# Storing the activation sums of a Strassen MLP in its up phase, loading operands in place, and moving the embedding projection between plain chunks

## The chip, the cores and the metric

One core of one Trainium2 chip. The metric is the device time of one execution of the program in microseconds (us). Three executions of the kernel before were timed.

## What is computed

One layer of a decoder trunk, for 512 tokens of width 2048, all in f32:

```
u  = rmsnorm(x);  x = x + gla(u)             # gated linear attention, 4 heads, output projection w_out
u  = rmsnorm(x);  z = relu(u @ w_up) ** 2    # 2048 -> 8192
x  = x + z @ w_down                          # 8192 -> 2048
u  = rmsnorm(x);  x = x + sigmoid(u @ w_ple_gate) * (p @ w_ple_proj)
out = rmsnorm(x)
```

`p` is an embedding of width 256 for each token. The GLA stage has its own input projections (q, k, v, output gate and a low-rank decay gate).

## The kernel before

**Arithmetic.** Every f32 operand is split into a high part in a reduced format (fp32r, a cast on ACT) and the remainder (a subtraction on DVE). A product is then three matmuls: high by high, high by remainder, remainder by high (mm3, L148 to L151). Weights are loaded by SP into a tile raw, cast on ACT to whi (L139) and subtracted on DVE to wlo (L141). The pools for these tiles have 3 raw, 4 whi, 4 wlo and 2 ld buffers; activations live in a pool of 34 slots of 4 KB per partition. The engines take their instructions in order, each from a queue of its own; a scheduler sets the order of the rows from the program's order.

**Stages**, by the trace: q, k and the low-rank gate of head 0 with the transposes of x (0 to 77 us); v, output gate, attention (to 652); the output projection wo, 8 groups of 4 weight chunks, whose results go through evac_out (L731 to L752; to 840); up (848 to 1503); the embedding projection and the first down groups (1503 to 1570); down (to 2230); the gate with the final norm (to the end).

**Start.** x_load (L242) loads 256 columns of x by SP; x_tile (L246) transposes 128 of them on PE. x_load(c+1) is issued when the tiles of x_load(c) are begun (L340).

**Output projection.** For each of 16 row tiles i, evac_out adds the residual xres (loaded by POOL from xT_d), writes the scaled u, adds the square to acc, stores h to DRAM (h_d), and builds the operands of the up phase for each pair kp of tiles: XS (sums) and XA (L709 to L725). The pairs 5 and 6 keep their u in a tile u_late, which is taken from the raw pool (L737) and held until after the projection.

**Up and down by a 2x2 Strassen scheme** with 7 products instead of 8. A weight chunk of 4 x 256 (chunk_sums, L796) gets its sums on DVE (L801, L804, L805); a chunk is 2 x 7 x 3 = 42 matmuls of 256 columns. In up there are 32 groups of 4 chunks; the 7 products of a group go to 4 banks and are added in combine (L825 to L836) into a tile e of 8 parts, of which 4 are the result. hidden (L838) applies Relu and Square and stores the four parts to DRAM (z_d, two stores by POOL).

Down works on slices of 4, 3, 3, 3, 3 chunks of the 16 that z has, as the slots hold no more; each slice has 8 groups g. Groups 0, 3 and 7 are PLAIN: ordinary products, 24 matmuls of 512 columns for each chunk (plain_chunk, L882); the others are Strassen groups. build (L896) makes the operands of one chunk: for two tiles kp it loads z into an ld buffer (POOL, L900), then hidden_operands (L867) casts z to Zh and subtracts to Zl, forms the four differences zd in the one tile d (L872 to L874), and splits these to Zdh and Zdl. After each group the partial h is loaded from h_d, added to and stored again (residual_in, L845, and residual_out, L852).

**The order around the change.** The main loop (L966 on) walks over the list work. At the first down chunk it builds the chunks 0 and 1 and runs the four parts of the embedding projection (project_embedding, L932; 4 x 24 matmuls; results leave through raw buffers named pp, copied by ACT at L941 and stored by ACT at L942). After group 2 of a slice one chunk of the next slice is built, where the slots allow; the rest is built chunk by chunk in group 0 of that slice. The steps that follow a group (combine, stores) are put into the list todo and flushed after the second chunk of the next one. rest_of_scale (L763) forms the token sums of acc (ps_ts_mlp) after the third up chunk.

Of the kernel before, what the change touches and what calls it, by code (L numbers as in the profile page):

```python
# [9 lines left out]
F32 = mybir.dt.float32  # L10
# [50 lines left out]
def trunk_kernel(ctx, tc, a, out):  # L61
# [63 lines left out]
    z_d = dram.tile([NG, P, 2, T], F32, name="z_d")  # L125
    pp_d = dram.tile([NTT, P, D], F32, name="pp_d")
# [184 lines left out]
    x_load(1)  # L311
    x_squares(0)
    ready = 2
    for k in range(NK):
# [351 lines left out]
    def spare_tile(shape, name):  # L666
        return mpool.tile(shape, F32, tag="d", name=name)

    def temp(name):
        return spare_tile([P, T], name)  # L670
# [4 lines left out]
    acc2 = mpool.tile([P, T], F32, tag="acc2", name="acc2")  # L675

# [51 lines left out]
    late = {}  # L728
    XOPS = [None] * NKP

    def evac_out(i, ps):  # L731
# [12 lines left out]
        h = late["x"][:, i % 2, :]  # L744
        nc.vector.tensor_tensor(out=h, in0=ps, in1=h, op=ALU.add)
        nc.vector.scalar_tensor_tensor(
            out=late["u"][:, i % 2, :], in0=h, scalar=vec("norm_mlp", i), in1=rb, op0=ALU.mult, op1=ALU.mult)
        add_squares(h, f"mlp_{i}", i == 0)
        if i % 2:
# [10 lines left out]
    f2 = mpool.tile([P, T], F32, tag="f2", name="f2")  # L760
    g2 = mpool.tile([P, T], F32, tag="g2", name="g2")

    def rest_of_scale():  # L763
        ssum = token_sums(acc2, "mlp")
        ms = tiny([P, NTT], "ms2")
        nc.vector.tensor_scalar(out=ms, in0=ssum, scalar1=1.0 / D, scalar2=EPS, op0=ALU.mult, op1=ALU.add)
        r = rstd_of(ssum, D, NTT, "mlp")
        f = tiny([P, NTT], "f")
        nc.vector.tensor_tensor(out=f, in0=r, in1=rinv, op=ALU.mult)
        ft = tiny([P, NTT], "ft")  # L770
        nc.vector.tensor_tensor(out=ft, in0=f, in1=f, op=ALU.mult)
        bcast(ft, f2, "f2")
# [23 lines left out]
    def chunk_sums(w, k4, g, name):  # L796
# [9 lines left out]
        return raw  # L806

# [17 lines left out]
    def combine(ps, name):  # L825
# [10 lines left out]
        return e[:, 0:4, :].rearrange("p (f h) t -> p f (h t)", f=2)  # L836

    def hidden(g, ps):  # L838
        z = combine(ps, f"up{g}")
        nc.scalar.activation(out=z, in_=z, func=AF.Relu)  # L840
        nc.scalar.activation(out=z, in_=z, func=AF.Square)
        for f in range(2):
            nc.gpsimd.dma_start(z_d[g, :, f, :], z[:, 1 - f, :])

    def residual_in(s_, g):  # L845
        hs = load([P, 2, T], f"h_{s_}_{g}")
# [5 lines left out]
    def residual_out(s_, g, hs):  # L852
        if s_ == len(SLICES) - 1:
            nc.vector.tensor_tensor(out=hs, in0=hs, in1=f2.unsqueeze(1).broadcast_to([P, 2, T]), op=ALU.mult)
        nc.gpsimd.dma_start(h_d[g], hs)

    def add_slice(s_, g, ps):
        z = combine(ps, f"dn{s_}_{g}")
# [275 lines left out]
```

## Time and profile before

| | |
|---|---|
| median of 3 executions | 2419.46 us (2417.47 to 2421.09) |
| the profiled execution | 2423.99 us, its span 2422.2 us |
| mean granted clock of TensorE | 0.984 of full speed |
| PE | busy 2361.6 us, 97% |
| DVE | busy 1690.2 us, 70% |
| ACT | busy 977.5 us, 40% |
| POOL | busy 152.5 us, 6% |
| DMA | 341.09 MB, 141 GB/s on the mean |

PE is TensorE, DVE is VectorE, ACT is ScalarE, POOL is GpSimd, SP is SyncE. PE's busy time holds matmuls of 256 and 512 columns; two may overlap in the records, so that the pace of a stretch is read from its length and its number of matmuls. An idle engine is of interest where PE waits for it.

### The profile page before, as it was taken

The numbers are of one execution on the slowest core, as the hardware profiler recorded it, in microseconds if no ns is written. First come the engines' busy times: TensorE is split into PE (matmuls) and PEld (weight loads), VectorE is DVE, ScalarE is ACT, GpSimd is POOL, SyncE is SP. The second block draws the span as 40 slices with busy tenths as digits, with TensorE's granted clock in tenths as the row PEclk, the third lists the DMA queues.
The fourth block names the chain that finished last, engine by engine and source line by source line (L and its number), as shares of the span: only waits on it lengthen the run. The fifth ranks groups of instructions, "written<-read, shape, count | busy, mean of one in ns | idle before, by whom it ended". The sixth has DMA issues, their size and how long they took to land.

```text
span 2422.2 us, 36477 instructions
## 1 busy us (share of the span) xinstructions
PE 2361.6 (97%) x14778; PEld 2136.3 (88%) x14778; DVE 1690.2 (70%) x2579; ACT 977.5 (40%) x1216; POOL 152.5 (6%) x282
## 2 busy tenths in 40 slices
PE   7999999999999899999999999899999999999998
PEld 6888888888878699999999998699898989899887
DVE  5654736547464588888888888578887888878435
ACT  4433424324332344444444446334433334434333
POOL 2000000000000000000000000000101010100000
PEclk8999999999999899999999999899999999999999
DMA  8333323332433344444444444545555565655433
GB/s 252 97 88 94 87 79 96 95 94 85 127 130 113 122 124 146 132 131 131 132 131 131 131 131 142 184 149 170 191 179 195 187 203 178 215 191 190 149 114 113
DMA packets 247753, 341.09 MB, mean 141 GB/s; under 512 B 13732, under 2 KB 202336, under 8 KB 247584
## 3 DMA queue, kind: packets, MB, share of 16 engines
q1 hardware_dynamic: 213072, 228.68, 31.0%
q0 software_dynamic: 30240, 105.75, 12.6%
q10 hardware_dynamic: 4272, 4.33, 0.6%
q8 instruction: 115, 1.88, 0.3%
q14 instruction: 54, 0.44, 0.1%
HBM read 281.05 MB, written 57.67 MB: 140 GB/s over the span
## 4 chain that ended last, share of the span: by engine, by line
PE 78%; issue 8%; DVE 5%; DMA 4%; ACT 1%; POOL 0%; ACTq 0%; DVEq 0%; POOLq 0%
PE ps_up L822 9%; PE ps_up L819 9%; PE ps_up L821 9%; PE ps_d L821 5%; PE ps_d L819 5%; PE ps_d L822 4%; DMA z<-z_d 3%; PE ps_wo L151 2%; PE ps_v L149 2%; PE ps_wo L149 2%; PE ps_v L150 2%; PE ps_og L150 2%; PE ps_v L151 2%; PE ps_og L149 2%; PE ps_og L151 2%
## 5 line engine op out<-in xcount | busy, mean ns | idle before, releaser
L811 ACT CAST whi_up<-raw_up 128x896 fp32r<-128x896 f32 x256 | 239.8, 940 | 317.5 <-PE ps_up L821 309.5
L813 DVE TENSOR_TENSOR wlo_up<-raw_up,whi_up 128x896 fp32r<-128x896 f32 x256 | 277.7, 1087 | 92.9 <-ACT whi_up L811 92.9
L819 PE MATMUL ps_up<-XS,whi_up 128*128 128x256 f32 x1024 | 290.4, 284 | 0.0
L821 PE MATMUL ps_up<-XS,whi_up 128*128 128x256 f32 x1024 | 290.4, 284 | 0.0
L822 PE MATMUL ps_up<-XS,wlo_up 128*128 128x256 f32 x1024 | 290.0, 284 | 0.0
L811 ACT CAST whi_d<-raw_dn 128x896 fp32r<-128x896 f32 x160 | 149.0, 942 | 241.1 <-PE ps_d L821 141.8
L819 PE MATMUL ps_up<-XA,whi_up 128*128 128x256 f32 x768 | 218.6, 285 | 3.7 <-ACT whi_up L811 3.7
L822 PE MATMUL ps_up<-XA,wlo_up 128*128 128x256 f32 x768 | 218.1, 284 | 0.5 <-DVE wlo_up L813 0.5
L821 PE MATMUL ps_up<-XA,whi_up 128*128 128x256 f32 x768 | 217.8, 284 | 0.0
L813 DVE TENSOR_TENSOR wlo_d<-raw_dn,whi_d 128x896 fp32r<-128x896 f32 x160 | 172.9, 1087 | 35.6 <-ACT whi_d L811 34.8
L819 PEld LDWEIGHTS ps_up<-XS,whi_up 128*128 128x128 f32 x1024 | 197.4, 193 | 0.0
L821 PEld LDWEIGHTS ps_up<-XS,whi_up 128*128 128x128 f32 x1024 | 197.3, 193 | 0.0
L822 PEld LDWEIGHTS ps_up<-XS,wlo_up 128*128 128x128 f32 x1024 | 197.1, 193 | 0.0
L821 PE MATMUL ps_d<-Zdl,whi_d 128*128 128x256 f32 x640 | 181.1, 283 | 0.0
L819 PE MATMUL ps_d<-Zdh,whi_d 128*128 128x256 f32 x640 | 181.1, 283 | 0.0
L822 PE MATMUL ps_d<-Zdh,wlo_d 128*128 128x256 f32 x640 | 181.1, 283 | 0.0
L150 PE MATMUL ps_d<-Zl,whi_d 128*128 128x512 f32 x384 | 151.9, 396 | 5.0 <-DVE Zl L876 5.0
L149 PE MATMUL ps_d<-Zh,whi_d 128*128 128x512 f32 x384 | 151.7, 395 | 3.9 <-ACT whi_d L139 2.2
L151 PE MATMUL ps_d<-Zh,wlo_d 128*128 128x512 f32 x384 | 151.5, 394 | 0.5 <-DVE wlo_d L141 0.5
L819 PEld LDWEIGHTS ps_up<-XA,whi_up 128*128 128x128 f32 x768 | 147.9, 193 | 4.2 <-ACT whi_up L811 3.9
L822 PEld LDWEIGHTS ps_up<-XA,wlo_up 128*128 128x128 f32 x768 | 148.0, 193 | 0.9 <-DVE wlo_up L813 0.8
L821 PEld LDWEIGHTS ps_up<-XA,whi_up 128*128 128x128 f32 x768 | 148.0, 193 | 0.2 <-issue 0.2
(345 smaller groups left out, 6057.9 us busy)
## 6 DMA issues: line engine op xcount, KB each, us to landing
raw_up<-in_w_up SPq DMA_DIRECT2D x128, 512.0 KB, 3.8
raw_dn<-in_w_down SPq DMA_DIRECT2D x80, 512.0 KB, 3.7
raw_d<-in_w_down SPq DMA_DIRECT2D x48, 512.0 KB, 3.8
h<-h_d POOLq DMA_DIRECT2D x40, 512.0 KB, 4.6
h_d<-h POOLq DMA_DIRECT2D x40, 512.0 KB, 3.0
raw_v<-in_gla_w_in SPq DMA_DIRECT2D x32, 512.0 KB, 3.8
raw_og<-in_gla_w_in SPq DMA_DIRECT2D x32, 512.0 KB, 3.7
raw_wo<-in_gla_w_out SPq DMA_DIRECT2D x32, 512.0 KB, 3.4
```

The source lines that it names most:

```text
L149: nc.tensor.matmul(ps, lhsT=wa[0], rhs=wb[0], start=first, stop=False)
L150: nc.tensor.matmul(ps, lhsT=wa[0], rhs=wb[1], start=False, stop=False)
L151: nc.tensor.matmul(ps, lhsT=wa[1], rhs=wb[0], start=False, stop=last)
L811: nc.scalar.copy(hi[:, 1:8, :], raw[:, q_, 1:8, :])
L813: nc.vector.tensor_tensor(out=lo[:, 1:8, :], in0=raw[:, q_, 1:8, :], in1=hi[:, 1:8, :].bitcast(F32), op=ALU.subtract)
L819: nc.tensor.matmul(dst, lhsT=hi[:, wb, :], rhs=xh, start=first and q_ == 0 and half == 0, stop=False)
L821: nc.tensor.matmul(dst, lhsT=hi[:, wb, :], rhs=xl, start=False, stop=False)
L822: nc.tensor.matmul(dst, lhsT=lo[:, wb, :], rhs=xh, start=False, stop=last and q_ == 1 and (b == 3 or half == 1))
```

## The change

- **Start.** x_load is one tile of x further ahead.
- **Output projection.** The tile u_late is gone: the pairs 5 and 6 are scaled in place in xres (pair 5 in a new buffer ld2), after h is stored. The square is taken before the scaling. The first raw tile of the up phase is loaded and summed at i = 13, ahead of the last groups' end. The tile f2 shares the buffer of acc.
- **Up.** After Relu and Square, hidden_sums forms the four differences on DVE in the free parts of e, and a third store per group puts them to a new DRAM tile zd_d (512 KB). todo gives out one step per chunk.
- **Operands.** hidden_operands is replaced by split: the load goes into the slot of the remainder, ACT casts it into the high part's slot, and DVE subtracts in place. The parts Zu (from z_d) and Zd (from zd_d) are built separately; the plain groups need Zu only. Builds for the next slice come after groups 2, 6 and 7; 32 more loads of 512 KB go by POOL.
- **Embedding projection.** Its part i comes after plain chunk i of the first down group, and its results leave through the ld and ld2 buffers.

The diff's core:

```diff
@@ start
-                if ready % 2 == 0 and ready // 2 + 1 < NK // 2:
-                    x_load(ready // 2 + 1)
+                if ready % 2 == 0 and ready // 2 + 2 < NK // 2:
+                    x_load(ready // 2 + 2)
@@ evac_out
-            late["x"] = load([P, 2, T], f"xres_{kp}")
+            late["x"] = (load2 if kp == 5 else load)([P, 2, T], f"xres_{kp}")
...
-            if kp == 5:
-                late["s"] = wtile([P, 2, 2, T], "raw", "u_late")
             if kp in (5, 6):
-                late["u"] = late["s"][:, kp - 5, :, :]
+                late["u"] = late["x"]
...
         if i % 2:
             nc.gpsimd.dma_start(h_d[kp], late["x"])
+            if kp in (5, 6):
+                for j in range(2):
+                    scale_out(i - 1 + j, late["x"][:, j, :])
+            if i == 13:
+                first_raw.append(raw_of(0))
@@ up
+    def hidden_sums(g, e):
+
+        for o, x, y in ((4, 2, 3), (5, 3, 1), (6, 2, 5), (7, 0, 6)):
+            nc.vector.tensor_tensor(out=e[:, o, :], in0=e[:, x, :], in1=e[:, y, :], op=ALU.subtract)
+        nc.gpsimd.dma_start(zd_d[g], e[:, 4:8, :])
@@ operands
+    def split(src, kp, name):
+
+        h, l = (slot([P, 4, HT], f"Z{name}{n}_{kp}", F32R) for n in ("h", "l"))
+        nc.gpsimd.dma_start(l.bitcast(F32), src)
+        nc.scalar.copy(h, l.bitcast(F32))
+        nc.vector.tensor_tensor(out=l, in0=l.bitcast(F32), in1=h.bitcast(F32), op=ALU.subtract)
+        return h, l
@@ main loop
-            if s_ == 0 and g == 0 and first:
-                for i in range(4):
-                    build_to(i // 2 + 1)
-                    project_embedding(i)
             if g == 0:
                 build_to(k4 + 1)
+            if g == 1:
+                build_sums_to(k4 + 1)
...
                 plain_chunk(ps, k4, g, first, last, f"{name}_{k4}")
+                if s_ == 0 and g == 0:
+                    flush()
+                    build_to(min(k4 + 2, end))
+                    project_embedding(k4)
+                    build_sums_to(k4 + 1)
...
-            if g == 2 and last and 8 * (SLICES[s_] + 1) <= 34:
-                build_to(end + 1)
+            if last and end < NG // 2:
+                if g == 2 and SLICES[s_] == 3:
+                    build_to(end + 2)
+                if g == 6:
+                    build_to(end + 3)
+                if g == 7:
+                    build_sums_to(end + 1)
         if todo and not first:
-            flush()
+            todo.pop(0)()
```

**ACT at the end of group 5 of the output projection** (sq_mlp are the squares that wait for the group's results, whi_wo6 the weight casts of the group that follows). Before:

```order
L682 ACTIVATE sq_mlp_8_5333<-xres_4_5328 128x512
L682 ACTIVATE sq_mlp_9_5338<-xres_4_5328 128x512
L714 CAST XS0_4_5342<-u_4_5330 128x1024
L722 CAST XA0_4_5344<-u_4_5330 128x256
L722 CAST XA0_4_5344<-u_4_5330 128x512
L682 ACTIVATE sq_mlp_10_5482<-xres_5_5477 128x512
L682 ACTIVATE sq_mlp_11_5487<-xres_5_5477 128x512
L722 CAST XA0_4_5344<-u_late_5479 128x256
L139 CAST whi_wo6_0_5495<-raw_wo6_0_5493 128x1024
L139 CAST whi_wo6_1_5525<-raw_wo6_1_5523 128x1024
```

With the change:

```order
L684 ACTIVATE sq_mlp_8_5333<-xres_4_5329 128x512
L684 ACTIVATE sq_mlp_9_5338<-xres_4_5329 128x512
L140 CAST whi_wo6_0_5495<-raw_wo6_0_5493 128x1024
L716 CAST XS0_4_5343<-u_4_5331 128x1024
L724 CAST XA0_4_5345<-u_4_5331 128x256
L724 CAST XA0_4_5345<-u_4_5331 128x512
L140 CAST whi_wo6_1_5525<-raw_wo6_1_5523 128x1024
L140 CAST whi_wo6_2_5555<-raw_wo6_2_5553 128x1024
L140 CAST whi_wo6_3_5585<-raw_wo6_3_5583 128x1024
L684 ACTIVATE sq_mlp_10_5481<-xres_5_5478 128x512
L684 ACTIVATE sq_mlp_11_5485<-xres_5_5478 128x512
```

The four casts of group 6 have moved ahead of the squares of pair 5.

**ACT in the embedding projection** (whi_wp are its weight casts, pp its results, Zh and Zdh the casts of operands; whi_d0_1_0_0 belongs to the first chunk of down group 1). Before:

```order
L942 DMA pp_d_110<-pp_0_1_13431 128x2x512
L139 CAST whi_wp1_13451<-raw_wp1_13449 128x1024
L841 ACTIVATE e_up31_13665<-e_up31_13665 128x1024
L871 CAST Zh_4_13679<-z_4_13676 128x1024
L875 CAST Zdh_4_13681<-zd_4_13678 128x1024
L871 CAST Zh_5_13693<-z_5_13690 128x1024
L941 COPY pp_1_0_13455<-ps_ple1_0_0_13456 128x512
```

With the change, at the projection's end:

```order
L978 COPY pp_3_1_13897<-ps_ple3_1_0_13898 128x512
L978 COPY pp_3_1_13897<-ps_ple3_1_1_13906 128x512
L911 CAST Zdh_6_13915<-Zdl_6_13916 128x1024
L979 DMA pp_d_111<-pp_3_1_13897 128x2x512
L844 CAST whi_d0_1_0_0_13934<-raw_dn1_0_13838 128x896
L844 CAST whi_d0_1_0_1_13959<-raw_dn1_0_13838 128x896
L911 CAST Zdh_7_13920<-Zdl_7_13921 128x1024
L911 CAST Zuh_8_15226<-Zul_8_15227 128x1024
L844 CAST whi_d0_1_1_0_13989<-raw_dn1_1_13925 128x896
```

Before, Zh and Zdh stand between the weight casts and the copies from the first part on; with the change the operands that the next chunk does not need stand at the end, around the casts of group 1.

**POOL from up to down** (z_d and zd_d are the stores of the last up groups, Zul and Zdl the loads into the slots). Before:

```order
L843 DMA z_d_109<-e_up30_13263 128x512 x2
L900 DMA z_2_13491<-z_d_109 128x1024
L900 DMA z_3_13505<-z_d_109 128x1024
L900 DMA z_4_13676<-z_d_109 128x1024
L900 DMA z_5_13690<-z_d_109 128x1024
L843 DMA z_d_109<-e_up31_13665 128x512 x2
L900 DMA z_6_13739<-z_d_109 128x1024
```

With the change:

```order
L910 DMA Zul_3_13598<-z_d_109 128x1024
L910 DMA Zdl_0_13645<-zd_d_110 128x1024
L876 DMA z_d_109<-e_up31_13576 128x512 x2
L910 DMA Zdl_1_13650<-zd_d_110 128x1024
L883 DMA zd_d_110<-e_up31_13576 128x1024
L910 DMA Zul_4_13685<-z_d_109 128x1024
L910 DMA Zul_5_13690<-z_d_109 128x1024
L910 DMA Zdl_2_13737<-zd_d_110 128x1024
L910 DMA Zdl_3_13742<-zd_d_110 128x1024
L910 DMA Zul_6_13777<-z_d_109 128x1024
L910 DMA Zul_7_13782<-z_d_109 128x1024
```

The loads of z go out as before around the last stores, and those of zd stand between them.

## Rows read from the trace of the kernel before

**Rows 1.** The page: the span, and PE's line of busy time, share and instructions.

```profile
span 2422.2 us, 36477 instructions
PE 2361.6 (97%) x14778; PEld 2136.3 (88%) x14778; DVE 1690.2 (70%) x2579; ACT 977.5 (40%) x1216; POOL 152.5 (6%) x282
```

**Rows 2.** Waits of PE: line, releaser: us in total, times, longest us.

```profile
PE ps_xT L249 <- DMA x<-in_x: 8.0, 3, 4.1
PE ps_ple L149 <- ACT whi_wp L139: 7.6, 3, 2.8
PE ps_wo L149 <- ACT whi_wo L139: 5.0, 2, 4.1
PE ps_d L150 <- DVE Zl L876: 5.0, 4, 2.2
PE ps_up L819 <- ACT whi_up L811: 3.7, 2, 2.6
PE ps_ts_mlp L215 <- DVE acc L683: 3.6, 1, 3.6
```

**Rows 3.** Stretches: us, busy (count) of PE, PEld, DVE, ACT, POOL, clock, DMA, GB/s.

```profile
51.20:59.40 8.20, 4.12 (x15) 3.12 (x14) 2.00 (x4) 2.12 (x7) 1.24 (x2) 0.50 0.81 265
145.30:193.80 48.50, 48.50 (x230) 40.87 (x229) 26.91 (x47) 17.64 (x21) 0.00 (x0) 1.00 0.27 76
787.50:800.50 13.00, 7.92 (x20) 5.61 (x19) 7.64 (x13) 4.60 (x6) 1.28 (x2) 0.61 0.48 161
840.20:855.20 15.00, 8.27 (x41) 7.87 (x41) 14.83 (x28) 6.82 (x11) 1.33 (x2) 0.66 0.33 105
858.00:1480.00 622.00, 622.00 (x5176) 621.02 (x5175) 508.60 (x788) 298.21 (x339) 33.57 (x62) 1.00 0.43 132
968.90:1017.30 48.40, 48.40 (x406) 48.40 (x405) 39.89 (x62) 22.80 (x27) 2.17 (x4) 1.00 0.40 123
1505.50:1551.00 45.50, 31.17 (x90) 22.24 (x89) 25.82 (x30) 23.05 (x29) 3.77 (x7) 0.77 0.67 221
1727.50:1735.50 8.00, 5.20 (x15) 3.62 (x14) 6.46 (x10) 2.94 (x4) 0.53 (x1) 0.79 0.42 142
1857.00:1865.00 8.00, 5.11 (x14) 3.50 (x14) 6.06 (x9) 3.04 (x4) 0.53 (x1) 0.79 0.50 171
```

**Rows 4.** SP's timeline, 33-51 us: start, us, operation, [idle before <- releaser].

```profile
33.22 14.87 SPq L137 DMA_DIRECT2D raw_v<-in_gla_w_in  x3
48.14 2.01 SPq L244 DMA_DIRECT2D x<-in_x  x3
```

**Rows 5.** DMAs: tile, engine, count, KB each, median us to landing.

```profile
x<-in_x SPq DMA_DIRECT2D x8, 512.0 KB, 7.5
z<-z_d POOLq DMA_DIRECT2D x32, 512.0 KB, 4.4
```

**Rows 6.** ACT's timeline at 790 us and at 847 us.

```profile
790.81 1.99 ACT L139 CAST whi_wo<-raw_wo 128x1024 fp32r<-128x1024 f32 x2
846.88 0.93 ACT L811 CAST whi_up<-raw_up 128x896 fp32r<-128x896 f32 x1
```

**Rows 7.** DVE's and ACT's timelines in the up phase, 1121 to 1124 us.

```profile
1121.68 1.09 DVE L813 TENSOR_TENSOR wlo_up<-raw_up,whi_up 128x896 fp32r<-128x896 f32 x1 [0.90 <-ACT whi_up L811]
1122.82 0.94 ACT L811 CAST whi_up<-raw_up 128x896 fp32r<-128x896 f32 x1 [1.18 <-PE ps_up L821]
```

**Rows 8.** By tile (zd, z, e_up): count: duration ns min/median/max, first and last start.

```profile
L873 DVE TENSOR_TENSOR zd<-z,zd x32: 415/419/427, 892.4 to 2111.0; 128x256 f32<-128x256 f32 x32
L900 POOL DMA_DIRECT2D z<-z_d x32: 528/528/548, 886.8 to 2106.0; - x32
L843 POOL DMA_DIRECT2D z_d<-e_up x64: 540/540/557, 880.7 to 1510.9; - x64
```

**Rows 9.** POOL's timeline at 1507 us.

```profile
1507.06 0.53 POOL L900 DMA_DIRECT2D z<-z_d  x1 [4.31 <-DVE Zl L876]
```

**Rows 10.** ACT's timeline at 1727 us.

```profile
1727.37 1.05 ACT L871 CAST Zh<-z 128x1024 fp32r<-128x1024 f32 x1 [3.95 <-DMA z<-z_d]
```

More of the change, by code (lines that the diff above doesn't have):

```diff
@@ L125, in trunk_kernel @@
     z_d = dram.tile([NG, P, 2, T], F32, name="z_d")
+    zd_d = dram.tile([NG, P, 4, HT], F32, name="zd_d")
     pp_d = dram.tile([NTT, P, D], F32, name="pp_d")
@@ L675, in trunk_kernel, with load2 @@
     acc2 = mpool.tile([P, T], F32, tag="acc2", name="acc2")
+    def load2(shape, name):
+        return mpool.tile(shape, F32, tag="ld2", name=name)
     def add_squares(src, name, first):
@@ L725, in operands, with chunk_sums, raw_of, scale_out @@
         return ops
+    w_up = a["w_up"].rearrange("o k c -> (o k) c")
+    w_dn = a["w_down"].rearrange("o k c -> (o k) c")
+    B11, T1, T3, B22, B21, T2, T4 = range(1, 8)
+    PRODUCTS = ((A11, B11), (R2, T2), (S3, T3), (S1, T1), (A12, B21), (R4, B22), (A22, T4))
+    BANK = ((0, 0), (0, 1), (1, 0), (1, 1), (2, 0), (2, 1), (3, 0))
+    def chunk_sums(w, k4, g, name):
+        raw = wtile([P, 2, 8, P], "raw", f"raw_{name}")
+        rows = raw.rearrange("p q (k b n) c -> p (q k) b (n c)", k=2, b=2)
+        nc.sync.dma_start(rows[:, :, 0, :], w_rows(w, 4 * k4, 4, 256 * g, 256))
+        tc.keep_in_program_order(nc.vector.tensor_tensor(
+            out=raw[:, :, 2:4, :], in0=raw[:, :, 1:5:3, :], in1=raw[:, :, 0:1, :].broadcast_to([P, 2, 2, P]),
+            op=ALU.add))
+        nc.vector.tensor_tensor(out=raw[:, :, 6, :], in0=raw[:, :, 2, :], in1=raw[:, :, 4, :], op=ALU.add)
+        nc.vector.tensor_tensor(out=raw[:, :, 7, :], in0=raw[:, :, 6, :], in1=raw[:, :, 5, :], op=ALU.add)
+        return raw
+    work = []
+    for g in range(NG):
+        for k4 in range(NK // 4):
+            work.append((0, g, k4, k4 == 0, k4 == NK // 4 - 1))
+    c0 = 0
+    for s_, nc_ in enumerate(SLICES):
+        for g in range(NKP):
+            for j in range(nc_):
+                work.append((1 + s_, g, c0 + j, j == 0, j == nc_ - 1))
+        c0 += nc_
+    def raw_of(n):
+        if n >= len(work):
+            return None
+        stage, g, k4, _, _ = work[n]
+        if stage == 0:
+            return chunk_sums(w_up, k4, g, f"up{g}_{k4}")
+        if g not in PLAIN:
+            return chunk_sums(w_dn, k4, g, f"dn{g}_{k4}")
     late = {}
     XOPS = [None] * NKP
+    first_raw = []
+    def scale_out(i, h):
+        nc.vector.scalar_tensor_tensor(
+            out=late["u"][:, i % 2, :], in0=h, scalar=vec("norm_mlp", i), in1=rb, op0=ALU.mult, op1=ALU.mult)
     def evac_out(i, ps):
@@ L745, in evac_out @@
         nc.vector.tensor_tensor(out=h, in0=ps, in1=h, op=ALU.add)
-        nc.vector.scalar_tensor_tensor(
-            out=late["u"][:, i % 2, :], in0=h, scalar=vec("norm_mlp", i), in1=rb, op0=ALU.mult, op1=ALU.mult)
         add_squares(h, f"mlp_{i}", i == 0)
+        if kp not in (5, 6):
+            scale_out(i, h)
         if i % 2:
             nc.gpsimd.dma_start(h_d[kp], late["x"])
+            if kp in (5, 6):
[3 more added lines that the diff above has]
+                first_raw.append(raw_of(0))
             if kp < 5:
@@ L757, in trunk_kernel @@
         XOPS[kp] = operands(kp, late[kp], late["w"][:, 4:8, :], "X")
[L760 removed]
+    F2 = []
     g2 = mpool.tile([P, T], F32, tag="g2", name="g2")
@@ L771, in rest_of_scale @@
         nc.vector.tensor_tensor(out=ft, in0=f, in1=f, op=ALU.mult)
-        bcast(ft, f2, "f2")
+        F2.append(mpool.tile([P, T], F32, tag="acc2", name="f2"))
+        bcast(ft, F2[0], "f2")
         gi_ = tiny([P, NTT], "gi")
@@ L893, in add_plain, with build_sums_to @@
         residual_out(s_, g, hs)
-    built = [0]
-    def build(kc):
-        for kp in (2 * kc, 2 * kc + 1):
-            u = load([P, 2, T], f"z_{kp}")
-            nc.gpsimd.dma_start(u, z_d[kp])
-            d = spare_tile([P, 4, HT], f"zd_{kp}")
-            hidden_operands(kp, u, d)
+    built = [0, 0]
     def build_to(n):
         while built[0] < min(n, NG // 2):
-            build(built[0])
-            built[0] += 1
+            for kp in (2 * built[0], 2 * built[0] + 1):
+                u = split(z_d[kp].rearrange("p k (h t) -> p (k h) t", h=2), kp, "u")
+                ZOPS[kp] = [None] * 4 + [(u[0][:, o, :], u[1][:, o, :]) for o in (0, 2, 3)]
+                for k in range(2):
+                    ZH[2 * kp + k] = [t[:, 2 * k:2 * k + 2, :].rearrange("p h t -> p (h t)") for t in u]
+            built[0] += 1
+    def build_sums_to(n):
+        while built[1] < min(n, NG // 2):
+            for kp in (2 * built[1], 2 * built[1] + 1):
+                d = split(zd_d[kp], kp, "d")
+                ZOPS[kp][:4] = [(d[0][:, o, :], d[1][:, o, :]) for o in range(4)]
+            built[1] += 1
     todo = []
@@ L934, in project_embedding @@
         for t2 in range(NTT // 2):
-            o = wtile([P, 2, 512], "raw", f"pp_{gi}_{t2}")
+            o = (load2 if (2 * gi + t2) % 3 == 2 else load)([P, 2, 512], f"pp_{gi}_{t2}")
             for t in range(2):
@@ L943, in project_embedding @@
                 pp_d[2 * t2:2 * t2 + 2, :, 512 * gi:512 * gi + 512].rearrange("t p c -> p t c"), o)
-    work = []
-    for g in range(NG):
-        for k4 in range(NK // 4):
-            work.append((0, g, k4, k4 == 0, k4 == NK // 4 - 1))
-    c0 = 0
-    for s_, nc_ in enumerate(SLICES):
-        for g in range(NKP):
-            for j in range(nc_):
-                work.append((1 + s_, g, c0 + j, j == 0, j == nc_ - 1))
-        c0 += nc_
-    def raw_of(n):
-        if n >= len(work):
-            return None
-        stage, g, k4, _, _ = work[n]
-        if stage == 0:
-            return chunk_sums(w_up, k4, g, f"up{g}_{k4}")
-        if g not in PLAIN:
-            return chunk_sums(w_dn, k4, g, f"dn{g}_{k4}")
-    raw_next = raw_of(0)
+    raw_next = first_raw[0]
     ps = None
```

50 lines of the change are left out of this document (12 added, 38 removed).

## The prediction

> **What bounds the kernel now.** I read the page first: PE is busy 97% of the span [rows 1], so every gain must be time in which PE stands still or runs at the lower clock; a shorter DVE or ACT stream is worth nothing by itself. Then the waits of PE [rows 2], each with the engine it waits for, and then the stretches around them [rows 3], because after a wait the granted clock falls, so a wait costs more than its own length. In two undisturbed stretches a matmul takes 48.50/230 = 0.211 us (512 columns) and 48.40/406 = 0.119 us (256 columns), granted clock 1.00, that is 2.4 GHz [rows 3]. What a stretch lost is its length less its matmuls at these rates. The whole up phase (858 to 1480 us) loses nothing: PE is busy in all of its 622.00 us [rows 3]. So the change can gain in four places only: the start, both ends of the output projection, the change from up to down, and the boundaries of the down slices.
>
> **A, the start.** Stretch 51.2 to 59.4: PE waits 4.1 us for a tile of x [rows 2], and has the clock 0.50 (1.2 GHz). Its 15 matmuls would take at most 15 × 0.211 = 3.2 us, so at least 5.0 of 8.2 us are lost [rows 3]. The cause is SP's order: three loads raw_v hold SP for 14.87 us (they wait for raw buffers), and the last three loads of x leave only behind them, at 48.14 [rows 4]; 48.14 + 7.5 us landing [rows 5] is the 55.7 at which PE goes on. With x one tile further ahead x_5 leaves ahead of raw_v. x_6 and x_7 still leave at 48; x_6 lands at some 55.6, and PE, which now has x_5, needs it one step of k later (12 matmuls of 0.211 and the transposes, about 4 us after 51.6). I take −5.0. Against it: x_2 now lands together with x_1. Bounds +1.5 (x_1 later by a fifth of a landing of 7.5) and −6.5.
>
> **B, the output projection.** Group 5 to 6 (787.5 to 800.5): 20 matmuls would take 4.2 us, 8.8 of 13.0 are lost [rows 3]; 4.1 of it is one wait for whi_wo [rows 2]. ACT's row order above shows why: whi_wo6_0 stands behind the squares of group 5, which wait for PE's last matmul, since u_late holds a raw buffer, so that the load of weights and its cast come late; ACT casts at 790.81 [rows 6]. With u_late gone all four casts stand ahead of these squares. All 8.8 go. Group 7 to up (840.2 to 855.2): 15.0 − 41 × 0.119 = 10.1 lost [rows 3], of which 3.6 are the matmul ps_ts_mlp waiting for acc and 3.7 whi_up [rows 2]. The chunk of 42 matmuls that now stands ahead of ps_ts_mlp lasts 5.0 us and covers the 3.6. But the cast for the second chunk still stands behind XS of the last pair; the cast at 846.88 [rows 6] feeds a PE that is through with the first chunk about 846: a gap of 2, and 0 to 4 for the clock. I leave 3.5: −6.7. **B together −15.5**, bounds −11 (the clock stays low and the gap is 6) and −19 (all goes).
>
> **C, the up phase pays.** Each of 32 groups gets four subtracts of 128x256 on DVE and one store of 512 KB on POOL. The same form takes 419 ns [rows 8], 4 × 0.42 = 1.7 us a group (less where it overlaps), and DVE's load rises from 508.60/622 = 82% to 82% + 1.7/20.1 = 90%. POOL gets 0.54 us more a group [rows 8], and is idle for most of one. The place that matters: the sums stand in DVE's queue just ahead of one weight remainder, wlo_up. In the present trace that one ends at 1122.77 [rows 7]. When is it needed? ACT's next cast waits for PE to free the buffer of four tiles back and begins at 1122.82 [rows 7]; PE then still has two tiles of 21 × 0.119 = 2.5 us ahead of it, so it needs it at about 1127.8: a margin of 5.0 us, and there was 0.90 us of idle time in front of it [rows 7]. 1.7 us fit: **C = 0**, bounds 0 and +3 (a delay in the last groups, where loads for the down phase stand in the queues too; nothing here shortens PE's work, so no gain). The combine of the next group also waits for the third store, 20 us earlier: covered.
>
> **D, up to down.** Stretch 1505.5 to 1551: 90 matmuls of 0.211 are 19.0, so 26.5 of 45.5 are lost, clock 0.77 [rows 3]. PE waits 7.6 us for whi_wp [rows 2]: the embedding's weight casts stand on ACT behind Zh and Zdh, and these behind loads of z that come one at a time, since a load waits until DVE has done with the buffer (4.31 us idle at POOL [rows 9]). Now the loads go into slots, and PE's order is plain chunk, embedding, plain chunk, embedding: eight pieces of 24 matmuls = 5.1 us, 41 us together, called T to T+41 from the end of up. Operands of chunk k are then needed at T + 10.1 k. POOL: Zu_0 to Zu_3 leave before T; the last group's combine and its three stores of 0.54 us, with two loads between them, bring POOL to some T+8.5 (in the present trace its last store starts at 1510.9 [rows 8], 10 us after up's last matmul); then eight loads, 8 × 0.53 us [rows 8], leave by T+12.4 and land 4.4 us later [rows 5] if alone; as 4.2 MB at the 221 GB/s of this stretch [rows 3] they need 19 us, so the last lands by T+27.5. Chunk 3 needs Zu_6 and Zu_7 at T+30.7. They fit. What is late next is the first chunk of group 1: its cast stands on ACT behind the last copy of the embedding (half of a 1.05 us cast [rows 10]), Zdh_6 (1.05), a DMA issue and itself (0.94 [rows 7]), some 3 us after PE is through; its second tile, behind Zuh_8, costs 1.5 more; the clock 2 to 4 after that. I leave 8: **D −18.5**, bounds −5 (in-order queues give most of it back) and −26.5.
>
> **E, slice boundaries.** 1727.5 and 1857: 8.0 − 15 × 0.211 = 4.8 and 8.0 − 14 × 0.211 = 5.0 lost [rows 3]; the other two boundaries have small parts of the 5.0 us that PE waits for Zl, longest 2.2 [rows 2], I take 1.2 for both. ACT's Zh idles 3.95 us for a load of z [rows 10] that left late, behind the store of h. Now the next slice's loads follow group 6, in slots that its last Strassen use frees, some 10 us ahead of use. **E −11**, bounds −5 (one boundary stays) and −11.5. The build's own sums leave DVE (3 operations per pair), worth nothing, as PE does not wait on them elsewhere.
>
> **The end (gate)** keeps its order on PE. Its acc tile now waits for the last use of f2, in the last down group; it is needed after the first gate group, 192 matmuls = 40 us later: 0.
>
> **The sum**: −5.0 − 15.5 + 0 − 18.5 − 11.0 = **−50**. The profiled execution took 2423.99 us (2422.2 span and 1.8 around it), so 2374; the median of the runs, 2419.46, is 4.5 below that execution: **2369**.
>
> **A rule against D and A.** What the rows show: a load takes 7.5 us to land in the first 50 us, with DMA at 0.81 there, and 4.4 us for z later [rows 3, 5]; loads that overlap slow each other. The Trainium skill, DMA: Bandwidth & Descriptors, section Issuing engines are not separate DMA queues, says that DMAs of all issuing engines run on the same 16 DMA engines and interleave. By that rule the burst on POOL would also delay the weights on SP; the trace agrees for x, and no run here shows the burst. The sum would by the rule be that of rival 2, by the rows at their medians that of the forecast.
>
> **The rivals.**
> 1. *The transition stall stays.* ACT and DVE take their queues in order, and Zd casts, which nobody needs before T+41, now stand between the embedding's casts and copies; a single late load then stops both. For it: this is how it stalls today [rows 9]. Against it: slots, not two buffers. D is −5 only: −50 + 13.5, **2383**.
> 2. *Transfers share the DMA engines.* In the burst, 8 loads and 5 weight loads are 6.8 MB, 31 us at 221 GB/s, from T+8.5: the last at T+39, 8 us late for chunk 3; and x gains nothing (+1.5): −50 + 8 + 6.5, **2384**.
> 3. *Everything goes.* No rest in B and D: −50 − 3.5 − 8, and the bounds of A and E at the other end, −2: about **2355**.
> 4. *The change does not free the raw buffer.* The first up chunk's raw tile is now taken during the last group of the output projection, as u_late was; two buffers are left for weights, and the 8.8 us stall moves from group 6 to group 7: **2378**.
> 5. *Slower.* One mechanism: DVE in the up phase. The four sums wait for ACT's Square, and wlo_up, the weight sums and the raw buffer that SP waits for stand behind them. It decides when the remainder comes later than its 5.0 us margin, and it must cost more than 50/31 = 1.6 us in each group to cancel the gains. If DVE at 90% loses 2.5 us a group: 31 × 2.5 = 78, so −50 + 78, **2447**. For it: 82% today and an in-order queue; against it: the margin and 0 us of waits in 622.
>
> **How the numbers follow.** Forecast 0.58, rivals in order 0.12, 0.08, 0.10, 0.07, 0.05. A measurement of this kernel tells 0.2%, 4.8 us. The range reaches from 2352 (rival 3, less 3 for the runs' spread) to 2394 (rivals 1, 2 and 4 with another bound, 10 us, on top); rival 5 is left out. Faster: all but rival 5 and a small share where two of the mishaps meet: 0.93; within 0.2%: 0.03; slower: 0.04.
>
> **What would show it.** In the profile after: no wait of PE for whi_wo over 1 us; ps_ts_mlp without a wait; x's wait at 55 us under 1 us; at the transition under 10 us lost, with clock above 0.9; no wait on Zl at slice starts; the up phase still without a PE gap. I am wrong if PE waits for wlo_up or whi_up in the up phase, if PE waits between the plain chunks, or if the clock falls at the start of group 1 for more than 4 us.

## The result, and the profile after

The changed kernel takes 2395.49 us (median of four executions, 2388.14 to 2398.97); the kernel before took 2420.28 us beside it. The ratio is 0.9894, 95% interval 0.9865 to 0.9922. It is faster by about 25 us, half of the 50 that the sum came to, and 1.5 us outside the range. Measured again on the chip that the record numbers 9, the two stood at 2390.12 and 2416.71 (ratio 0.9888, 0.9873 to 0.9903).

The page of the profiled execution (2398.36 us), its span and its first row, to be held against [rows 1]; PE has the same 14778 matmuls in a span 25.6 us shorter, and POOL, with 64 more DMAs, 186.5 us of work instead of 152.5:

```profile
span 2396.6 us, 36734 instructions
PE 2350.1 (98%) x14778; PEld 2132.5 (89%) x14778; DVE 1690.5 (71%) x2611; ACT 974.6 (41%) x1216; POOL 186.5 (8%) x346
```

The waits of PE in the changed kernel (line, releaser: us in total, times, longest us), against [rows 2]:

```profile
PE ps_d L852 <- ACT whi_d L844: 7.2, 3, 3.6
PE ps_lr L304 <- ACT lr_w L335: 6.0, 1, 6.0
PE ps_xT L250 <- DMA x<-in_x: 4.9, 2, 3.9
PE ps_wo L150 <- ACT GH L602: 3.6, 1, 3.6
PE ps_d L150 <- ACT Zuh L911: 2.6, 1, 2.6
PE ps_up L852 <- ACT whi_up L844: 1.8, 1, 1.8
```

The waits of before for whi_wp, whi_wo (4.1), ts_mlp and Zl are gone, as forecast, and that for whi_up has halved. x keeps 4.9 of its 8.0 us. But two stand here that were not there before at all, lr_w and GH, and they lie in stages in which the prediction expected either a gain or nothing. whi_d has grown from 2.2 us to 7.2. The wait for Zuh stands between the plain chunks, where the prediction said that it would be wrong if PE waited.

To place the time, the program is cut at the first matmul of each stage. The columns are the lengths of the stages in us, read from the timelines of PE; "before" and "changed" are the profiles that belong to the two times above; the other two are later profiles of the same kernels on chip 9.

| stage (from first matmul to first matmul) | before | changed | difference | forecast | before, chip 9 | changed, chip 9 | difference |
|---|---|---|---|---|---|---|---|
| A: start to v | 86.1 | 86.8 | +0.8 | -5 | 84.5 | 85.9 | +1.4 |
| v to output projection | 566.5 | 566.5 | 0.0 | 0 | 566.4 | 566.4 | 0.0 |
| B: output projection to up | 195.3 | 186.1 | -9.2 | -15.5 | 195.4 | 183.9 | -11.5 |
| C: up | 652.7 | 652.1 | -0.6 | 0 | 652.7 | 651.7 | -1.0 |
| D: end of up to down group 3 | 109.5 | 101.1 | -8.5 | -18.5 | 110.5 | 96.8 | -13.7 |
| E: down group 3 to gate | 614.4 | 606.6 | -7.8 | -11 | 609.3 | 604.7 | -4.6 |

Stretches of the changed kernel, with the columns of [rows 3] (us, busy and count of PE, PEld, DVE, ACT, POOL, granted clock, DMA share, GB/s):

```profile
20.90:29.10 8.20, 2.25 (x6) 1.16 (x4) 0.36 (x2) 0.81 (x5) 0.55 (x1) 0.50 0.99 283
655.80:672.10 16.30, 12.66 (x41) 10.03 (x40) 8.64 (x22) 4.21 (x7) 4.51 (x9) 0.69 0.63 224
838.80:853.80 15.00, 13.20 (x98) 13.00 (x97) 14.66 (x28) 6.82 (x11) 1.31 (x2) 0.89 0.32 107
849.00:1471.00 622.00, 622.00 (x5171) 621.04 (x5170) 549.93 (x908) 299.39 (x341) 48.66 (x90) 1.00 0.50 156
1497.80:1508.70 10.90, 10.90 (x49) 9.01 (x49) 8.01 (x12) 6.05 (x8) 4.84 (x9) 1.00 0.62 182
1491.50:1537.00 45.50, 41.66 (x175) 33.44 (x174) 26.15 (x28) 27.14 (x34) 6.62 (x13) 0.96 0.80 290
1537.00:1560.00 23.00, 16.02 (x87) 14.38 (x86) 16.23 (x22) 11.28 (x14) 3.53 (x7) 0.86 0.61 220
```

Of these, the third (the step to up, 98 matmuls where 41 were done) and the fourth (up, no gap at all with DVE at 549.93/622 = 88%) are as forecast. The first two are the new stalls. The fifth is an undisturbed piece of the alternation, with matmuls of 512 columns alone: 10.90/49 = 0.222 us for one, 0.227 by the starts of 24 (1497.84 to 1503.28). The last two are the change from up to down: 173 such matmuls, 39.3 us of 45.5, and then the start of group 1, in which PE is busy 16.02 of 23.00 us, at 0.86 of the clock.

**The new stall at the start.** The low-rank weights are loaded by ACT's own queue. Rows of ACT's timeline:

```profile
14.10 1.06 ACT L140 CAST whi_qk<-raw_qk 128x1024 fp32r<-128x1024 f32 x1 [2.56 <-DMA raw_qk<-in_gla_w_in]
14.13 0.45 ACTq L327 DMA_DIRECT2D lr_raw<-in_gla_w_in  x1
28.41 1.29 ACT L335 CAST lr_w<-lr_raw 128x128 fp32r<-128x128 f32 x6 [7.39 <-DMA lr_raw<-in_gla_w_in]
```

The load leaves at 14.13, behind a cast of a weight tile, and takes 14.2 us to land; before, it left at 10.58 and landed in 4.4. The same load and the same cast in the profile before:

```profile
10.58 0.40 ACTq L325 DMA_DIRECT2D lr_raw<-in_gla_w_in  x1
14.14 1.05 ACT L139 CAST whi_qk<-raw_qk 128x1024 fp32r<-128x1024 f32 x1 [0.79 <-DMA raw_qk<-in_gla_w_in]
```

The cast begins at the same time in both (14.14 and 14.10). What has moved is the order on ACT's queue: the load stood ahead of this cast, and with the change it stands behind it. So it also left ahead of x_1 before, and leaves behind x_1 and x_2 now. SP's rows, before and with the change:

```profile
11.93 0.50 SPq L244 DMA_DIRECT2D x<-in_x  x1
```

```profile
11.72 1.05 SPq L245 DMA_DIRECT2D x<-in_x  x2
```

Now PE reaches the low-rank matmuls first and waits 6.0 us.

**The new stall in the output projection.** Rows of POOL's timeline, and one of ACT's:

```profile
654.21 0.74 POOL L785 DMA_DIRECT2D xres<-xT_d  x1 [31.18 <-PE ps_o L615]
654.95 2.68 POOL L597 DMA_DIRECT2D gr<-gated_d  x5
```

```profile
659.24 0.62 ACT L602 CAST GH<-gr 128x512 fp32r<-128x512 f32 x1 [8.70 <-DMA gr<-gated_d]
```

POOL stands idle for 31.18 us ahead of a load of xres. It is the one of pair 5, which the change gives the buffer ld2. The scheduler found a free buffer and put the load between the second and the third of the twelve loads gr. But ld2 is opened where the attention stage has just given up its memory, and by the row's releaser the load waits for ps_o at L615, the matmul that reads att_diag last. Ten loads gr stand behind it; the casts GH, the squares behind these on ACT, and then PE wait.

### The profile page after: what moved, and what is told of

Same layout as the page of the kernel before. It is cut to its first block, busy times and chain, and to the rows that moved or that the text cites. A ratio compares the mean times of both kernels' runs of the same rounds, so it can differ in the third digit from the quotient of the medians.

```text
span 2396.6 us, 36734 instructions
## 1 busy us (share of the span) xinstructions
PE 2350.1 (98%) x14778; PEld 2132.5 (89%) x14778; DVE 1690.5 (71%) x2611; ACT 974.6 (41%) x1216; POOL 186.5 (8%) x346
## 4 chain that ended last, share of the span: by engine, by line
PE 87%; issue 6%; DMA 4%; DVE 1%; ACT 1%; POOL 0%; ACTq 0%; POOLq 0%; SPq 0%; DVEq 0%
PE ps_up L852 9%; PE ps_up L855 9%; PE ps_up L854 9%; PE ps_d L855 6%; PE ps_d L852 5%; PE ps_d L854 5%; PE ps_d L151 3%; PE ps_d L152 3%; PE ps_d L150 3%; PE ps_v L150 2%; PE ps_wo L150 2%; PE ps_v L151 2%; PE ps_og L150 2%; PE ps_v L152 2%; PE ps_og L152 2%
## 5 line engine op out<-in xcount | busy, mean ns | idle before, releaser
L846 DVE TENSOR_TENSOR wlo_d<-raw_dn,whi_d 128x896 fp32r<-128x896 f32 x160 | 172.4, 1087 | 29.0 <-ACT whi_d L844 28.3
L150 PE MATMUL ps_d<-Zuh,whi_d 128*128 128x512 f32 x384 | 150.4, 392 | 2.6 <-ACT Zuh L911 2.6
L151 PE MATMUL ps_d<-Zul,whi_d 128*128 128x512 f32 x384 | 150.3, 392 | 1.3 <-DVE Zul L912 1.3
L152 PE MATMUL ps_d<-Zuh,wlo_d 128*128 128x512 f32 x384 | 150.0, 391 | 0.0
```

The costliest lines, as they stand in the source:

```text
L150: nc.tensor.matmul(ps, lhsT=wa[0], rhs=wb[0], start=first, stop=False)
L151: nc.tensor.matmul(ps, lhsT=wa[0], rhs=wb[1], start=False, stop=False)
L152: nc.tensor.matmul(ps, lhsT=wa[1], rhs=wb[0], start=False, stop=last)
L846: nc.vector.tensor_tensor(out=lo[:, 1:8, :], in0=raw[:, q_, 1:8, :], in1=hi[:, 1:8, :].bitcast(F32), op=ALU.subtract)
```

## The experiments

The runs stand on two chips: the pin of xres_5, the first part undone, x_5 alone and the pin of h alone ran on chip 13, all others, the base among them, on chip 9. The base is the changed kernel. The kernel before took 2417.37 us beside the runs on chip 13, and 2416.71 on chip 9 (2415.63 beside the last three runs). So each time is compared by its distance to the kernel before that ran beside it.

**The changed kernel again, as the base** (no edit).

> The changed kernel, unaltered, beside the others on one chip, as their common base. Its first profile has 6.0 us of waiting for lr_w, 3.6 for GH at 656 and 2.6 for Zuh at 1514; the first two come from the order of the rows and should be there again in any execution, the size of the third depends on how loads land and may move by some us. Expected 2388 to 2397, and between 25 and 30 us under the kernel before.

Measured 2390.12 (2388.63 to 2392.70), 26.6 under the kernel before: this is the distance that the other runs are held against. PE waits 6.4 us for lr_w, 3.6 for GH and 2.9 for Zuh: the first two stalls belong to the program, not to one execution.

**The load of xres_5 behind the loads gr.**

```diff
-            nc.gpsimd.dma_start(late["x"], xT_d[i:i + 2].rearrange("k p t -> p k t"))
+            ld_x = nc.gpsimd.dma_start(late["x"], xT_d[i:i + 2].rearrange("k p t -> p k t"))
+            if kp == 5:
+                tc.keep_in_program_order(ld_x)
```

> The changed kernel, with one row of POOL's queue moved: the load of xres_5 (the pair that now has the buffer ld2) is pinned behind the twelve loads gr of the output projection instead of standing between the second and the third. Theory 1 (head of the queue): in the changed kernel that load waits for the last read of att_diag, whose memory ld2 takes over, and holds the ten loads behind it; pinned, PE's wait of 3.64 us for GH at 656 goes, and the stretch 652 to 680 is about 8 us shorter: some 2387 to 2388 against 2395.5. Rival: the loads gr land late because the queue of DMAs is fuller, whatever their order; then PE's wait for GH stays and the time stays within 2 us of the changed kernel.

Measured 2382.63, 34.7 under the kernel before, 8.1 more than the base. Output projection to up takes 178.7 us instead of 183.9 (195.4 before). The loads gr leave one by one from 622.67 on, the last five at 653.00, as in the kernel before, and the stretch runs at full clock; a stretch of this kernel:

```profile
653.50:670.00 16.50, 16.45 (x73) 12.57 (x73) 11.70 (x29) 6.25 (x10) 2.18 (x5) 1.00 0.33 112
```

The head of the queue it was. 5.2 of the 8.1 us lie in this stage (the three other runs on chip 13, without the pin, have 183.0 to 185.0 there); the rest is spread over other stages, within what executions differ.

**The first part of the change undone.**

```diff
-    x_load(2)
...
-                if ready % 2 == 0 and ready // 2 + 2 < NK // 2:
-                    x_load(ready // 2 + 2)
+                if ready % 2 == 0 and ready // 2 + 1 < NK // 2:
+                    x_load(ready // 2 + 1)
```

> The changed kernel with the first part of the change undone: x is loaded one tile ahead, as before. Theory 1: the first part gained nothing, since the 6.0 us that PE waits for the low-rank weights lr_w (their load stands on ACT's queue behind a cast that now comes later, and lands in 14 us beside two loads of x) take back the 4 to 5 us that it saves at 51 us; undone, the wait for lr_w goes, the wait of 4.1 us for x at 52 us is back, and the time is that of the changed kernel within 3 us. Theory 2 (as predicted, the late lr_w is an accident of one execution): undone it costs 5 us.

Measured 2388.23, 29.1 under the kernel before, 2.5 more than the base. The intervals of the two ratios overlap (0.9862 to 0.9891 here), so the time alone says only that the first part did not give 5. The stage says more: the start takes 84.2 us, with the part 86.6 and 87.0 in two profiles of the same chip, so the part cost a little. The wait for lr_w is gone, that for x is back (4.2 us). Theory 1 holds but for one step: the cast that it names does not come later (14.10 and 14.14 above), the load has moved behind it.

**Only x_5 early.**

```diff
-    x_load(2)
...
-                if ready % 2 == 0 and ready // 2 + 2 < NK // 2:
-                    x_load(ready // 2 + 2)
+                if ready % 2 == 0 and ready // 2 + 1 < NK // 2:
+                    c = ready // 2 + 1
+                    for cc in {4: (4, 5), 5: ()}.get(c, (c,)):
+                        x_load(cc)
```

> The changed kernel, with x_5 alone loaded early (together with x_4, ahead of the loads raw_v) and the other loads of x as before. If theory 1 of the start holds (the cost comes from x_2 beside x_1, the gain from x_5 ahead of raw_v), neither the wait for lr_w nor that for x_5 is there: 5 to 6 us faster than the changed kernel, about 2390. If the wait at 51 us has another cause, it is within 2 us of the kernel that has the first part undone.

Measured 2386.31, 31.1 under the kernel before, 4.5 more than the base; the start takes 80.9 us, 5.0 less than in the base and 3.4 less than with the part undone. lr_raw leaves at 10.65, ahead of x_1 again, lands in 4.8 us, and neither wait is there (the longest for x is 1.7). So a gain at 51 us was there to be had, and what ate it came with the early loads of x: with them lr_raw leaves later, and has x_1 and x_2 ahead of it. This run takes away both, so it does not tell whether the place on ACT's queue or the bytes of x cost more.

**The sums and the third store alone**, in the kernel before: hidden_sums and its store after each up group, read by nothing, with todo giving out one step per chunk as in the change; down forms its own sums.

> The kernel before, with one part of the change alone: the four differences and the third store of every up group. Nothing reads what is stored; down forms its own sums as before. The prediction put this part at 0 (bounds 0 and +3), since the sums fit into a margin of 5.0 us ahead of PE. Expected: the kernel before within 3 us, and no wait of PE in the up phase. Rival (DVE at 90% of the up phase becomes late): waits for wlo_up or whi_up in the groups, 31 times some tenth of a us or more, 5 us and upwards.

Measured 2416.47 against 2416.71, ratio 1.000 (0.999 to 1.001). The whole up phase, a stretch of this kernel:

```profile
860.00:1482.00 622.00, 622.00 (x5176) 620.98 (x5175) 549.14 (x905) 299.40 (x342) 50.38 (x93) 1.00 0.50 158
```

DVE has 549.14 us of work instead of 508.60 [rows 3], and PE has no gap: the term C = 0 stands.

**The loads of h for groups 2 and 5 pinned.** In the changed kernel the transition's rows on POOL are these:

```profile
1502.39 1.11 POOL L876 DMA_DIRECT2D z_d<-e_up  x2 [20.01 <-ACT e_up L874]
1505.12 0.54 POOL L883 DMA_DIRECT2D zd_d<-e_up  x1 [1.03 <-DVE e_up L882]
1505.72 1.14 POOL L910 DMA_DIRECT2D Zul<-z_d  x2
...
1536.81 0.53 POOL L887 DMA_DIRECT2D h<-h_d  x1 [20.22 <-DMA pp_d<-pp]
1537.41 1.12 POOL L910 DMA_DIRECT2D Zdl<-zd_d  x2
```

The load of h_0_2 also goes to ld2, and waits 20.22 us for the store of an embedding result, with Zdl_6 and Zdl_7 behind it (which load of h a row is follows from the program's order, as the rows carry no numbers).

```diff
-        nc.gpsimd.dma_start(hs, h_d[g])
+        ld_h = nc.gpsimd.dma_start(hs, h_d[g])
+        if g % 3 == 2:
+            tc.keep_in_program_order(ld_h)
```

> The changed kernel, with the loads of h for groups 2 and 5 of each slice (those that take ld2) pinned in program order in POOL's queue. In the changed kernel h_0_2 stands ahead of the loads Zdl_6, Zdl_7 and Zul_8 and waits 20.2 us at POOL for the store of an embedding result. Theory 1 (head of the queue): pinned, these three leave some 20 us earlier, PE's waits for whi_d at 1541 (3.6 us) and 1552 (2.8 us) shrink to under 2 us each, with the slow clock behind them, and 5 to 8 us go: about 2389. Rival (order on ACT, as the prediction had it: the casts of group 1 come after the last copies of the embedding anyway): PE's wait at 1541 stays above 3 us and at most 4 us go, those of the second wait.

Measured 2390.21, 27.2 under the kernel before, as good as the base. PE's wait for whi_d (the last number, at the start of group 1) in the base and with the pin:

```profile
PE ps_d L852 <- ACT whi_d L844: 2.8, 2, 2.5
```

```profile
PE ps_d L852 <- ACT whi_d L844: 3.2, 2, 2.5
```

It is 2.5 us in both. The theory of the queue's head falls here: the place on POOL was not what this wait hung on. The rival, the order on ACT, is what is left, though its bound of 3 us was taken from the first profile and the base stands under it as well.

**The two repairs together.**

> The changed kernel with the two repairs of the first runs together: the load of xres_5 pinned behind the loads gr, and x_5 alone loaded early. If the two causes are separate, their gains add: about 6 to 8 us for the first and 5 for the second, 11 to 13 under the changed kernel on the same chip, about 2378. If the second gain was only time that the first wait hid or returned, the sum is 8 or less.

Measured 2378.15, 38.6 under the kernel before, 12.0 more than the base, on its chip. Alone the two gave 8.1 and 4.5: they add, within what executions differ.

**Zd one chunk later**, on top of the two repairs.

```diff
                     project_embedding(k4)
-                    build_sums_to(k4 + 1)
+                    build_sums_to(k4)
```

> The kernel with the two repairs, and the parts Zd in the first down group built one chunk later (none at the first plain chunk, the last in group 1). POOL then sends Zul_4 to Zul_7 ahead of Zdl_1 to Zdl_5, and on ACT the first two weight casts of group 1 stand ahead of the last embedding copies and of Zdh_6. Theory 1 (order: what is needed later stands ahead of what is needed now): PE's wait for Zuh before plain chunk 2 (about 2 us, 4 with what follows it) and that for whi_d at the start of group 1 (2.5 us and 0.6 for wlo_d) both fall under 1 us, 4 to 7 us off the kernel with the two repairs. Rival (the loads share the DMA engines, and the order does not help): the wait for Zuh stays within 1 us of what it was, and at most 3 us go, those of whi_d.

Measured 2376.20, only 2 less. The wait for Zuh is gone and none at the start of group 1 is over 1.4 us, so far as theory 1 has it, but the stretch takes as long as before (95.8 us), since a wait of 5.0 us has taken their place. That wait of PE, the row of DVE and those of POOL behind it, in this kernel:

```profile
PE ps_d L858 <- DVE wlo_d L849: 6.0, 3, 5.0
```

```profile
1539.21 1.23 DVE L892 TENSOR_TENSOR h<-h,g 128x1024 f32<-128x1024 f32 x1 [6.47 <-DMA h<-h_d]
```

```profile
1522.61 0.53 POOL L890 DMA_DIRECT2D h<-h_d  x1 [20.18 <-ACT pp L981]
1533.29 0.54 POOL L890 DMA_DIRECT2D h<-h_d  x1 [8.93 <-ACT whi_d L847]
```

DVE stands 6.47 us at the multiplication of h, with the weight remainders of group 1 behind it. The load that it waits for, h_0_0, left POOL at 1533.29 after 8.93 us of idling there, 10.7 us behind h_0_2; what made it late is what the next run asks.

**Both: Zd later and the loads of h pinned.**

> The kernel with Zd one chunk later, with the loads of h for groups 2 and 5 pinned as well. With Zd later, the waits for Zuh and whi_d went and one of 5.0 us for wlo_d, in the second half of group 1's first chunks, took their place: DVE stands at the multiplication of h_0_0, whose load left POOL 9 us late. If h_0_2's place in POOL's queue is what made it late, the wait of 5.0 falls by 2 us or more and the kernel is 2 to 5 us faster, about 2372. If it is the buffer (h_0_0 takes the one that an embedding result leaves by a store of some 9 us), the wait stays above 4 us and the time within 1.5 us.

Measured 2371.11 (2370.48 to 2373.64); ratio to the kernel before 0.9811 (0.9793 to 0.9830). It is the fastest of all, 44.5 us under the kernel before where the base is 26.6. Its stretches, the first 45.5 us of the transition and the next 23:

```profile
1476.40:1521.90 45.50, 44.70 (x200) 36.48 (x198) 29.27 (x34) 29.63 (x38) 7.52 (x14) 1.00 0.86 313
1521.90:1545.00 23.10, 20.77 (x164) 19.70 (x163) 20.20 (x31) 12.08 (x16) 2.67 (x5) 1.00 0.74 250
```

200 and 164 matmuls at clock 1.00, where the changed kernel had 175 and 87 in its two. From the end of up to group 3 it takes 88.9 us (96.8 in the base), and the longest wait for wlo_d is 1.2 us. The pin alone gave nothing, Zd later alone 2; together 6 to 7. Two queues stood one behind the other, and each hid the other.

**The last embedding results through the tile of combine**, on top of that, so that h_0_0 and h_0_1 need not wait for their stores.

```diff
...
+            if gi == 3:
+                if t2 == 0:
+                    both = wide("pp_3")
+                o = both[:, 4 * t2:4 * t2 + 4, :].rearrange("p (c h) t -> p c (h t)", c=2)
...
```

> The kernel of the run before in this list, with the last embedding results leaving through the tile of combine, which is idle there, so that the loads of h_0_0 and h_0_1 do not wait for their stores. Theory (the buffer): no wait of PE over 2 us is left between the plain chunks and the end of group 1, the stretch from up to down loses 8 us or less instead of 12 to 13, and the kernel is 3 to 6 us faster than the one with Zd one chunk later: 2370 to 2373. Rival (the next thing in a queue takes its place again, as it did twice): the loss of the stretch stays at 11 us or more.

Measured 2388.64: 17.5 slower than without it. PE waits 12.4 us for whi_d in three places, the longest 5.9:

```profile
PE ps_d L855 <- ACT whi_d L847: 12.4, 3, 5.9
```

With the buffers free, the scheduler puts the loads of h_0_0, h_0_1 and h_0_3, the multiplications and the store of h_0_0 ahead of the last Zd on POOL and ahead of weight sums on DVE. The rival holds, more strongly than it was put. The first of the waits can be followed back in the rows of POOL, DVE and ACT:

```profile
1512.99 0.53 POOL L890 DMA_DIRECT2D h<-h_d  x1 [19.85 <-ACT pp L988]
```

```profile
1519.27 1.23 DVE L894 TENSOR_TENSOR h<-h,g 128x1024 f32<-128x1024 f32 x1 [7.76 <-DMA h<-h_d]
```

```profile
1525.35 0.94 ACT L847 CAST whi_d<-raw_dn 128x896 fp32r<-128x896 f32 x1 [0.57 <-DVE raw_dn L748]
```

A load of h leaves after 19.85 us of idling at POOL, DVE stands 7.76 us at its multiplication, the weight sums stand behind that on DVE, and the first cast whi_d of group 1 waits for them. How much each of these rows cost, beside the casts Zdh that ACT waits for in the same time, was not separated.

**The kernel before once more, with a profile** (no edit).

> The kernel before, unaltered, for a second profile of it. The prediction read 4.8 and 5.0 us of lost time at the first two slice boundaries from a profiled execution that was 4.5 us above the median; the run with the sums alone, whose down phase is the same, showed 1.5 and 1.5 there. Theory 1: these losses come and go with how loads of z land, and an ordinary execution (some 2415 to 2417) shows 2 to 4 us less of them than the first profile. Theory 2: the run with the sums alone was the odd one; this profile shows 8 us or more at the two boundaries again.

Measured 2415.03; its profiled execution took 2418.18. PE waits 3.6 us for Zl, against 5.0 in the first profile [rows 2]:

```profile
PE ps_d L150 <- DVE Zl L876: 3.6, 3, 1.7
```

Group 3 to gate takes 609.3 us, against 614.4. With the sums alone it is 606.6. Theory 1 holds: in this stage, for which the first profile promised 11 us, 5 to 8 come and go with the execution. What sets them was not followed further.

## Why the prediction came out at half, and what of it held

**A failed.** "Against it: x_2 now lands together with x_1" priced the cost by x_1's own landing (+1.5). That step was wrong: x_1 lands no later (in 7.4 us in both profiles), and what was late was a third load, lr_raw on ACT's queue. It leaves 3.5 us later, as its row now stands behind a cast that it stood ahead of, and lands in 14.2 us instead of 4.4. The wait for x at 55.9 us is gone, as forecast (x_5 alone early leaves 3.4 us of gain over the start undone), and the 6 us of wait for lr_w take it back.

**B was right in both of its terms, and missed a row.** With xres_5 pinned the stage falls from 195.4 to 178.7, 16.7 for the forecast 15.5: the 8.8 at group 6 went whole, and the step to up keeps 15.0 - 98 × 0.119 = 3.3 us by the stretch above, where 3.5 were left. (About 1 us of the 16.7 is only moved: the matmuls ts_mlp now stand behind the first ones of up.) What failed is the step that followed the new buffer ld2. The prediction asked what u_late had held, not where on POOL the load into the new buffer would now stand. The order of the changed program shows xres_5 among the loads gr; only its memory and the queue behind it had to be looked at. It cost 5.2 us against the base and 7.4 against the first profile (186.1 - 178.7), as a wait that took the place of the one removed.

**C was right.** No gap in 622 us, and the part alone gives a ratio of 1.000.

**D had the mechanism, and two steps too small.** The alternation works: at 0.227 us for a matmul, 6.2 of the first 45.5 us are lost where 25.1 were. The rate was a little off: the stretch from which 0.211 us came held narrower matmuls of the attention as well, so that the 26.5 us that could be gained were 25.1. "The stores of the last group bring POOL to some T+8.5": the last store left at 1505.12, T+13.6, with T at 1491.5, and the prediction's own row had a last store 10 us after up's last matmul. "They fit" was shown for the last of the eight loads and chunk 3; Zul_4 left at T+14.2, landed some 10 us later and was cast at 1515.77, where PE had been done with the part before at 1514:

```profile
1515.77 1.04 ACT L911 CAST Zuh<-Zul 128x1024 fp32r<-128x1024 f32 x1 [2.40 <-DMA Zul<-z_d]
```

That is 2.6 us of wait, and by estimate some 2 of slow clock behind it. The rest at group 1 was put at 3 and 1.5 us, with a clock of 2 to 4, 8 in all; the profile has waits of 3.6 and 2.8 there, and of the 23.0 us from 1537 on some 10.8 are lost (66 matmuls of 256 columns and 19 of 512 begin there, 12.2 us at full pace). In the second pair of profiles D came to -13.7, so that 5 of the 10 us that are missing are this execution's or this chip's; the wait of 2.8 is part of it, as the base has 0.3 there. Rival 1 named the mechanism (Zd, which nobody needs yet, stands in front on in-order queues), and the runs bear it out: with Zd later and h pinned D gives 110.5 - 88.9 = 21.6. Rival 2 (the DMA engines are shared) is not excluded as a part: Zul lands in 6.5 us on the median where z took 4.4 [rows 5], and at 290 GB/s instead of 221. But with the order mended the bytes flow at 313 GB/s and PE is idle for 0.8 of the 45.5 us, so the order decides most of it. The Trainium skill, DMA: Bandwidth & Descriptors, section Issuing engines are not separate DMA queues, says that DMAs of all issuing engines share the same 16 DMA engines and interleave; the 6.5 us for Zul agree with it.

**E was sized on a bad draw.** The waits for Zl are gone, as forecast, but the size of the term was wrong. The 11 us came from one profile whose time stood 4.5 us above the median, as the prediction itself says; it subtracted from the median a gain that the median execution does not hold. In the second profile the stage is 5.1 us shorter, and the change gains 4.6 there. Over all profiles the stage takes 606.6 to 614.4 us where the change's operands are not in use (three) and 603.1 to 607.6 where they are (ten): about 5 us on the mean, and the 7.8 of the first pair are in part luck.

Rivals 4 and 5 did not come: PE waits 1.0 us for whi_wo in the whole output projection, and up has no gap. With all the edits of order together, one of which the change does not have (Zd later), the time is 2371.11, near the forecast of 2369; the median before is 4 us lower there.

By the first profiles the misses are 5.8 (A), 6.3 (B's new wait), 10.0 (D) and 3.2 (E), less 0.6 in C, together 24.7. The prediction's sum against its own execution was 2374; the execution came to 2398.36.

## What to carry to other kernels

A change of one load can move the rows of another on a queue that the change does not name (lr_raw). A tile that is given a new buffer is a new place in a queue: before costing the gain, find the row of its load in the changed order, and ask what its memory waits for and what stands behind it. On in-order queues a load ahead of its need is not free, and two queues in series have to be mended together before either shows anything. A gain read from one profile should be checked against how far that execution stands above the median, and whether the stall that is to go is what made it longer.

## What was not expected of the hardware

A load of 128 KB on ACT's queue (lr_raw) took 4.1 to 4.8 us to land in the nine profiles in which it left at 10.1 to 11.0, ahead of x_1, and 13.7 to 14.7 us in the four in which it left at 13.6 to 14.3, behind x_1 and x_2. Busy DMA engines alone do not make it slow: their share is full by the profile from 11 to 21 us in the kernel before, where it landed in 4.4 (left at 10.58), and from 14.1 to 28.3 with the change, where it took 14.2 (the profile gives 1.06 for both). Its 128 KB are pieces of 16 numbers, one from each row of the weight. Whether the pieces, the place behind x or the bytes in flight set the 14 us was not separated.
